# Output projection into up projection: weight tiles kept for both column halves, residual seeded in PSUM, first up operands made earlier

## The chip, the cores and the metric

The kernel runs on one core of one Trainium2 chip. A core has a matrix engine (PE, TensorE), three elementwise engines (DVE is VectorE, ACT is ScalarE, POOL is GpSimd), a queue engine (SP) that issues transfers, an on-chip memory of 128 partitions (SBUF) and an accumulator memory in eight banks (PSUM) into which PE writes. The metric is device time in microseconds (us). Before the change three timed runs gave 2550.85, 2553.93 and 2555.95 us; the median is 2553.93 us.

## What is computed

Two encoder layers over 1040 frames (16 learned ones and 1024 of input) of 1024 features, in fp32. Each layer has a mixing part and a gated feed-forward part:

```python
h = h + jnp.concatenate([o_gla, o_fox], axis=-1) @ w_out[i]
h = h + conv_ffn(rms_norm(h, ffn_norm[i]), w_up[i], conv_w[i], conv_b[i], w_down[i])
```

`conv_ffn` multiplies by `w_up` (1024 to 2 x 2816 columns), applies a causal convolution of width 3 to every column, gates one half by `silu` of the other, and multiplies by `w_down` (2816 to 1024). The change lies at the seam of the two lines: the last part of `@ w_out`, the RMS norm, and the first products with `w_up`.

## The kernel before, in words

**Layout.** Features lie on the 128 partitions, frames along the free dimension. The 1024 features are eight tiles `hT[0..7]` of 128 x 1040. Every product is made of three PE passes (`mm3`, lines 241 to 243): an fp32 operand is split into a rounded part `hi` (a cast on ACT) and the rest `lo` (a subtraction on DVE), and `hi*hi`, `lo*hi` and `hi*lo` are added up in PSUM. So every weight tile is loaded (SP, line 199), cast on ACT (line 208) and subtracted on DVE (line 210) before PE can use it; in the up projection the same is done in lines 1060 and 1061.

**The turn.** `ffn_up` begins with the output projection. Its frames are done in two halves `h = 0, 1` of 520 columns (516 and 524 in the last layer), each as two chunks of 260 (258). Eight output tiles `m` go through a half in the order of `orders`. For `m < 4` (`NSPLIT`) seven of the eight K tiles were already added during attention, so one K tile is left (6 matmuls); for `m >= 4` all eight are to be done (48 matmuls) and the residual comes from `hT[m]`. PE runs in program order. After the matmuls of one tile, `wout` adds the residual on DVE (line 1141), stores the tile (POOL, 1142), squares it on ACT (1144, 1147), adds the squares into `acc` on DVE (1148) and, in half 1, forms `gt` on ACT (1152) and `dd` on DVE (1154).

`scale(h)` sums `acc` over the partitions on PE (line 1118, tile `ssq`) and makes the reciprocal root (lines 296, 302 on ACT, 303 to 305 on DVE). `scale(0)` stands after the second tile of half 1; `scale(1)` stands after the first up product. `first_operand(k)` makes the normalised tile `k` of half 0 (DVE, 1124), and `put` splits it (ACT 1084, DVE 1085) into the operands `X[1]` (tiles 0 to 3) and `X[2]` (tiles 4 to 7).

**The up projection** is a seven-product block scheme: pairs of column blocks `j` with products `p = 1..7`. The list `seq` gives PE's order; it begins (0,2), (0,1), (1,2), (1,1), (2,2), (2,1), (0,6). Each entry is 24 matmuls. `X[2]` serves p = 2, `X[1]` p = 1; `X[6]`, `X[7]`, `X[4]`, `X[5]`, `X[3]` are made later from half 1 (`make_t2` and its neighbours, lines 1188 to 1222), all on DVE and ACT. `ensure(i)` makes the split weight operands of the entries up to `i + AHEAD` (`AHEAD` is 4).

**Buffers.** `Rings` hands out ten weight buffers w0 to w9 under three tags. While `stream` is set, `raw` turns over w0, w1, `hi` over w2 to w5 and `lo` over w6 to w9; otherwise `raw` has w0 to w3, `lo` w4 to w6, `hi` w7 to w9. The flag is cleared when the last output tile is written into the program (half 1, position 7, `m = 7`). Two output tiles (5 and 6) are kept split from half 0 to half 1 in buffers of the pool `fw`; the other six are loaded and split once per half. The entry of `seq` at an even place takes its split from `Rings`, that at an odd place from `fw`. Counting the turns of the rings in the program: the last two split chunks of `m = 7` in half 1 lie in w4 and w8, w5 and w9, and the first up operand, (0,2), takes w9 for `hi` and w4 (first layer) or w5 (second layer) for `lo`.

Larger operands lie in 39 slots of 128 x 1040 (33, and 6 more in the feed-forward part), which are handed out in the order in which they were returned. The order of the instructions on ACT, DVE, POOL and SP is made by a scheduler from readiness and program order; PE keeps the program's order.

Of the kernel before, what the change touches and what calls it, by code (L numbers as in the profile page):

```python
# [11 lines left out]
F32R = mybir.dt.float32r  # L12
BF16 = mybir.dt.bfloat16
AF = mybir.ActivationFunctionType
ALU = mybir.AluOpType
# [9 lines left out]
KD = D // 128  # L25
# [15 lines left out]
M_GK, M_GQ, M_GV, M_GR, M_REM, M_FQ, M_FK, M_FV, M_WO, M_UP = 0, 2, 4, 8, 12, 13, 17, 21, 25, 33  # L41
# [52 lines left out]
class Rings:  # L94


    def __init__(self, pool):
        self.pool, self.next, self.stream = pool, {}, False
        self.tags = {"raw": range(4), "lo": range(4, 7), "hi": range(7, 10)}, \
                    {"raw": range(2), "hi": range(2, 6), "lo": range(6, 10)}  # L100

    def tile(self, shape, dtype, tag, name, bufs=None):
        key = tag, self.stream
# [49 lines left out]
class Kern:  # L153
# [36 lines left out]
    def weights(self, src, slots=None, keep=None, vec=False):  # L190
        nc = self.nc
        nk = src.shape[1]
        parts = []
        if slots:
            HI, LO = slots
        for k0 in range(0, nk, 4):
            n = min(4, nk - k0)
            raw = self.wp.tile([128, 4, 128], F32, tag="raw", name="raw", bufs=4)
            nc.sync.dma_start(raw[:, :n, :], src[:, k0:k0 + n, :])
            if slots:  # L200
                hi, lo = HI[:, k0:k0 + 4, :], LO[:, k0:k0 + 4, :]
# [6 lines left out]
            nc.scalar.copy(hi[:, :n, :], raw[:, :n, :])  # L208
            eng = nc.gpsimd if self.att and not vec else nc.vector
            eng.tensor_tensor(out=lo[:, :n, :], in0=raw[:, :n, :], in1=hi[:, :n, :].bitcast(F32), op=ALU.subtract)  # L210
            for k in range(n):
                parts.append((hi[:, k, :], lo[:, k, :]))
        return parts
# [850 lines left out]
    def ffn_up(self, lyr, mix, hT, pp, fw, halves, o0, during_last):  # L1064
        nc, s = self.nc, self.slots
        W = halves[2]
        n = W // 2
        sl = [slice(c, c + W) for c in halves[:2]]
# [34 lines left out]
        def ensure(i):  # L1103
            while len(ops) < min(i + AHEAD + 1, len(seq)):
                ops.append(self.up_operand(lyr, *seq[len(ops)], fw, raws, len(ops) % 2))
# [19 lines left out]
            put(1 + k // 4, k % 4, h)  # L1125
        turn = {1: (), 3: (4, 5), 4: (6,), 5: (7, 0), 6: (1,), 7: (2, 3)}

        def wout(i, h):
            m = orders[h][i]
            k0 = KD - 1 if m < NSPLIT else 0  # L1130

            def f(w):
                if h == 1 and i == KD - 1:
                    self.wp.stream = False
                    ensure(0)
                ps = bank2("wo", (0, 1, 2, 0, 1, 3, 2, 1)[i] if h else i % 4)
                for k in range(len(w)):
                    for c in range(2):
                        self.mm3(ps[:, c, :n], w[k], mix[k0 + k], halves[h] + c * n, n, k == 0, k == len(w) - 1)
                x = hT[m][:, sl[h]]  # L1140
                nc.vector.tensor_tensor(out=two(x), in0=used(ps), in1=two(x), op=ALU.add)
                nc.gpsimd.dma_start(self.hm[m][:, sl[h]], x)
                if i == 0:
                    nc.scalar.activation(acc[:, sl[h]], x, AF.Square)
                else:
                    t = half(sq, i % 2)
                    nc.scalar.activation(t, x, AF.Square)
                    nc.vector.tensor_tensor(out=acc[:, sl[h]], in0=acc[:, sl[h]], in1=t, op=ALU.add)
                if h == 0:
                    return  # L1150
                if m < NSPLIT:
                    nc.scalar.mul(half(gt, m % 2), x, gain(m))
# [12 lines left out]

        def wout_weights(h, i):
            m = orders[h][i]
            if m in kept:
                return kept.pop(m)
            w = self.weights(self.wm[lyr, M_WO + m][:, KD - 1 if m < NSPLIT else 0:KD, :], keep=keep.get(m))  # L1170
            if m in keep:
                kept[m] = w
            return w
        todo = [(h, i) for h in range(2) for i in range(KD)]
        ahead = wout_weights(*todo[0])
# [2 lines left out]
            wout(this[1], this[0])(w)  # L1178
        for x in mix:
            s.put(*x)  # L1180
        s.put(gt)

        lowk, highk, t0, t1 = hT[:4], hT[4:], sl[0], sl[1]

# [578 lines left out]
```

## Time and profile before

| | before |
|---|---|
| median of three runs | 2553.93 us |
| the profiled execution's own time | 2549.59 us |
| its span | 2547.7 us |
| PE busy | 2483.9 us (97% of the span) |
| DVE busy | 1748.1 us (69%) |
| ACT busy | 1273.1 us (50%) |
| granted TensorE clock, mean | 0.994 |
| half 1 of the output projection, layer 0 | 551.3 to 577.8 us of the span |
| the same, layer 1 | 1811.4 to 1837.7 us |

A row of the timeline reads: start, duration, engine, line and operation, output tile, input tiles and shape, and in brackets how long the engine had stood idle before it and what ended that. A row of the windows view gives, for a stretch of the span, the busy time of each engine with its instruction count, the granted TensorE clock and the load of the transfers. The profiled execution lies 4.3 us below the median of the timed runs.

### The profile page before, as it was taken

Reading aid. Unit: us, or ns where it says so; the run is one execution under the profiler, and the core shown is the slowest. Engines: PE = TensorE matmul, PEld = TensorE weight load, DVE = VectorE, ACT = ScalarE, POOL = GpSimd, SP = SyncE. Lnnn points to the kernel's source line nnn. Section 1 sums busy time; section 2 is a strip of 40 time slices with the busy share of each in tenths; the row PEclk is TensorE's granted clock in tenths of the full one; section 3 lists DMA queues with packets and bytes.
Section 4 is the critical chain, followed back from the end, with each engine's and each line's share of the span. In section 5 each row is a group of like instructions: output and inputs, shape, how many; then the busy total and the mean of one; then the engine's idle time right before and its main releaser. Section 6 shows DMA issues by size and latency. Waiting matters only on the chain.

```text
span 2547.7 us, 48524 instructions
## 1 busy us (share of the span) xinstructions
PE 2483.9 (97%) x19278; PEld 2420.5 (95%) x19278; DVE 1748.1 (69%) x3389; ACT 1273.1 (50%) x2582; POOL 405.1 (16%) x580
## 2 busy tenths in 40 slices
PE   8999999999999999999999999999999999999998
PEld 7989999998999999999999899999999999999997
DVE  7655676769877777853565666777697777777535
ACT  7346666646544445641343466665464444455412
POOL 4033333210000000100210333331100000001002
PEclk9999999999999999999999999999999999999999
DMA  3232134342322224764312222142523222258622
GB/s 122 71 86 73 39 95 129 114 152 78 107 86 78 81 80 127 201 161 116 106 50 72 74 79 68 66 148 95 169 74 110 75 76 87 76 158 187 187 70 76
DMA packets 118515, 260.91 MB, mean 102 GB/s; under 512 B 14880, under 2 KB 32544, under 8 KB 118288
## 3 DMA queue, kind: packets, MB, share of 16 engines
q1 hardware_dynamic: 95136, 184.36, 23.2%
q0 software_dynamic: 22432, 72.71, 10.4%
q8 instruction: 151, 2.47, 0.4%
q10 hardware_dynamic: 720, 0.74, 0.1%
q14 instruction: 76, 0.62, 0.1%
HBM read 177.16 MB, written 67.81 MB: 96 GB/s over the span
## 4 chain that ended last, share of the span: by engine, by line
PE 65%; issue 17%; DVE 11%; DMA 3%; ACT 3%; POOL 1%; SPq 0%; DVEq 0%; POOLq 0%; ACTq 0%
PE mm L241 8%; PE mm L243 7%; PE mm L242 7%; PE up L242 5%; PE up L241 5%; PE up L243 5%; PE down L241 5%; PE down L242 5%; PE down L243 5%; PE av L741 3%; PE tr L723 2%; DVE P L694 2%; DVE x L1085 1%; PE wo L241 1%; PE S L686 1%
## 5 line engine op out<-in xcount | busy, mean ns | idle before, releaser
L241 PE MATMUL up<-x,hi 128*128 128x260 f32 (+1 forms) x2464 | 699.2, 284 | 8.0 <-ACT hi L1060 4.9
L243 PE MATMUL up<-x,hi 128*128 128x260 f32 (+1 forms) x2464 | 698.0, 283 | 2.1 <-DVE x L1085 2.1
L242 PE MATMUL up<-x,lo 128*128 128x260 f32 (+1 forms) x2464 | 698.5, 283 | 1.3 <-DVE lo L1061 1.3
L241 PEld LDWEIGHTS up<-x,hi 128*128 128x128 f32 x2464 | 466.6, 189 | 9.7 <-ACT hi L1060 5.3
L243 PEld LDWEIGHTS up<-x,hi 128*128 128x128 f32 x2464 | 467.0, 190 | 3.0 <-DVE x L1085 2.9
L242 PEld LDWEIGHTS up<-x,lo 128*128 128x128 f32 x2464 | 466.5, 189 | 2.0 <-DVE lo L1061 1.8
L1061 DVE TENSOR_TENSOR lo<-raw,hi 128x512 fp32r<-128x512 f32 x364 | 247.6, 685 | 173.4 <-ACT hi L1060 173.4
L241 PE MATMUL mm<-xh,hi 128*128 128x348 f32 (+4 forms) x1056 | 363.4, 344 | 0.0
L243 PE MATMUL mm<-xl,hi 128*128 128x348 f32 (+4 forms) x1056 | 340.0, 322 | 0.0
L242 PE MATMUL mm<-xh,lo 128*128 128x348 f32 (+4 forms) x1056 | 339.5, 321 | 0.0
L1060 ACT CAST hi<-raw 128x512 fp32r<-128x512 f32 x364 | 224.3, 620 | 145.5 <-PE up L243 84.9
L241 PEld LDWEIGHTS mm<-xh,hi 128*128 128x128 f32 x1056 | 200.0, 189 | 6.3 <-issue 5.3
L242 PEld LDWEIGHTS mm<-xh,lo 128*128 128x128 f32 x1056 | 200.0, 189 | 0.6 <-issue 0.3
L243 PEld LDWEIGHTS mm<-xl,hi 128*128 128x128 f32 x1056 | 198.8, 188 | 0.9 <-issue 0.7
L208 ACT CAST hi<-raw 128x512 fp32r<-128x512 f32 (+2 forms) x184 | 106.6, 582 | 185.0 <-PE down L243 113.0
L242 PE MATMUL down<-ah,lo 128*128 128x260 f32 (+1 forms) x704 | 198.0, 281 | 0.6 <-DVE lo L210 0.5
L243 PE MATMUL down<-al,hi 128*128 128x260 f32 (+1 forms) x704 | 198.1, 281 | 0.0
L241 PE MATMUL down<-ah,hi 128*128 128x260 f32 (+1 forms) x704 | 198.0, 281 | 0.0
L367 DVE TENSOR_TENSOR PT<-tr,PT 116x464 fp32r<-116x464 f32 (+3 forms) x240 | 122.3, 515 | 71.3 <-ACT PT L366 69.2
L702 ACT ACTIVATE P<-P,m 116x924 f32<-116x924 f32 (+4 forms) x144 | 110.5, 767 | 75.0 <-DVE m L694 69.4
L723 PE MATMUL tr<-ident,P 116*116 116x116 f32 x704 | 144.0, 268 | 2.3 <-DVE m L694 1.8
L1268 POOL DMA_DIRECT2D actd<-cv x44 | 23.6, 536 | 766.5 <-DVE cv L1267 745.5
(283 smaller groups left out, 5768.3 us busy)
## 6 DMA issues: line engine op xcount, KB each, us to landing
raw<-in_wm_dram SPq DMA_DIRECT2D x330, 256.0 KB, 2.9
raw<-in_wd_dram SPq DMA_DIRECT2D x64, 256.0 KB, 3.7
actd<-cv POOLq DMA_DIRECT2D x22, 520.0 KB, 3.0
actd<-cv POOLq DMA_DIRECT2D x22, 512.0 KB, 3.1
cb<-cd SPq DMA_DIRECT2D x16, 520.0 KB, 4.2
st<-actd SPq DMA_DIRECT2D x14, 520.0 KB, 5.1
st<-actd SPq DMA_DIRECT2D x14, 512.0 KB, 5.9
kA<-kA SPq DMA_DIRECT2D x24, 260.0 KB, 4.4
```

The costliest lines, as they stand in the source:

```text
L208: nc.scalar.copy(hi[:, :n, :], raw[:, :n, :])
L241: nc.tensor.matmul(ps, wh, xh[:, c0:c0 + n], start=first, stop=False, skip_group_check=more)
L242: nc.tensor.matmul(ps, wl, xh[:, c0:c0 + n], start=False, stop=False, skip_group_check=more)
L243: nc.tensor.matmul(ps, wh, xl[:, c0:c0 + n], start=False, stop=last, skip_group_check=more)
L367: nc.vector.tensor_tensor(out=lo, in0=src, in1=hi.bitcast(F32), op=ALU.subtract)
L686: nc.tensor.matmul(S[:rows, :n], q["qA"][e][:, qs], q["kA"][e][:, c0:k1], start=True, stop=False)
L694: nc.vector.tensor_tensor_reduce(out=x, in0=S[:rows, :n], in1=cb[:rows, c0:k1], scale=1.0, scalar=(BIG if ci == 0 else m[:rows, ci - 1:ci] ...
L702: nc.scalar.activation(x, x, AF.Exp, scale=-1.0, bias=low, accum_out=(den if nch < 3 else d2[:rows, 0:1]))
L723: nc.tensor.transpose(tr[:w, j, :rows], P[:rows, o:o + w], id_)
L741: nc.tensor.matmul(av[:, a:width], w.rearrange("p a b -> p (a b)"), x, start=(t == 0 and i == 0), stop=(t == last and i == 1))
L1060: nc.scalar.copy(hi[:, :nk, :], src[:, :nk, :])
L1061: nc.vector.tensor_tensor(out=lo[:, :nk, :], in0=src[:, :nk, :], in1=hi[:, :nk, :].bitcast(F32), op=ALU.subtract)
```

## The change

Four edits in the turn, and none elsewhere.

1. In half 0 every output weight tile is split once and kept. Tiles 0 to 3 (one K tile each) go into a slot of their own (`own`), tiles 5 and 6 into the pool `fw` as before, tiles 4 and 7 stay in the rings, which nothing else uses then. Half 1 loads and splits nothing.
2. `Rings.leave_stream` is called at the start of half 1. It gives the other layout from the ages of the buffers: `raw` gets the two raw buffers and the two `lo` buffers of tile 4, `hi` one `hi` buffer of tile 4 and both of tile 7, `lo` the other `hi` buffer of tile 4 and both `lo` buffers of tile 7.
3. The up operands (0,2) and (0,1) are written into the program at position 2 of half 1, after tile 4, and the next three at position 7.
4. For the full tiles (`m >= 4`) of half 1 the residual is copied by ACT into the PSUM banks before the matmuls (`seed`), which then add onto it. The addition of line 1141 on DVE is gone for them; the square, `dd` and a copy back into `hT` (ACT) read PSUM.

```diff
+FIRST_OPS = {2: 2, 7: 5}
...
+    def leave_stream(self):
+
+        age = {}
+        for t, ids in self.tags[True].items():
+            i = self.next.get((t, True), 0)
+            age[t] = [ids[(i + k) % len(ids)] for k in range(len(ids))]
+            self.next.pop((t, False), None)
+        (r0, r1), (h0, h1, h2, h3), (l0, l1, l2, l3) = age["raw"], age["hi"], age["lo"]
+        self.tags[False] = {"raw": [r0, r1, l0, l1], "hi": [h0, h2, h3], "lo": [h1, l2, l3]}
+        self.stream = False
...
+        place_out, seeds = (0, 1, 2, 0, 1, 3, 2, 1), {}
+        own = s.get(F32R, "wk", (128, 2 * NSPLIT, 128))
+
+        def seed(i):
+            ps = seeds[i] = bank2("wo", place_out[i])
+            nc.scalar.copy(used(ps), two(hT[orders[1][i]][:, sl[1]]))
...
             def f(w):
-                if h == 1 and i == KD - 1:
-                    self.wp.stream = False
-                    ensure(0)
-                ps = bank2("wo", (0, 1, 2, 0, 1, 3, 2, 1)[i] if h else i % 4)
+                if h == 1 and i == 0:
+                    self.wp.leave_stream()
+                if h == 1 and i in FIRST_OPS:
+                    ensure(FIRST_OPS[i] - AHEAD - 1)
+                if h == 1 and i + 1 < KD and orders[1][i + 1] >= NSPLIT:
+                    seed(i + 1)
+                ps, seeded = seeds.pop(i, None), h == 1 and m >= NSPLIT
+                if not seeded:
+                    ps = bank2("wo", place_out[i] if h else i % 4)
...
                 x = hT[m][:, sl[h]]
-                nc.vector.tensor_tensor(out=two(x), in0=used(ps), in1=two(x), op=ALU.add)
-                nc.gpsimd.dma_start(self.hm[m][:, sl[h]], x)
+                if not seeded:
+                    nc.vector.tensor_tensor(out=two(x), in0=used(ps), in1=two(x), op=ALU.add)
+                y = used(ps) if seeded else two(x)
...
-                    nc.scalar.activation(t, x, AF.Square)
+                    nc.scalar.activation(two(t), y, AF.Square)
                     nc.vector.tensor_tensor(out=acc[:, sl[h]], in0=acc[:, sl[h]], in1=t, op=ALU.add)
+                if seeded:
+                    nc.scalar.copy(two(x), y)
+                nc.gpsimd.dma_start(self.hm[m][:, sl[h]], x)
...
-                    nc.vector.scalar_tensor_tensor(out=diff(m - 4), in0=x, scalar=gain(m), in1=half(gt, m % 2),
+                    nc.vector.scalar_tensor_tensor(out=two(diff(m - 4)), in0=y, scalar=gain(m), in1=two(half(gt, m % 2)),
                                                    op0=ALU.mult, op1=ALU.subtract)
...
             m = orders[h][i]
-            if m in kept:
+            if h:
                 return kept.pop(m)
-            w = self.weights(self.wm[lyr, M_WO + m][:, KD - 1 if m < NSPLIT else 0:KD, :], keep=keep.get(m))
-            if m in keep:
-                kept[m] = w
+            src = self.wm[lyr, M_WO + m]
+            if m < NSPLIT:
+                w = self.weights(src[:, KD - 1:KD, :], [own[:, j:j + 1, :] for j in (m, NSPLIT + m)])
+            else:
+                w = self.weights(src, keep=keep.get(m))
+            kept[m] = w
             return w
```

More of the change, by code (lines that the diff above doesn't have):

```diff
@@ L98, in __init__ @@
         self.pool, self.next, self.stream = pool, {}, False
-        self.tags = {"raw": range(4), "lo": range(4, 7), "hi": range(7, 10)}, \
-                    {"raw": range(2), "hi": range(2, 6), "lo": range(6, 10)}
+        self.tags = [{"raw": range(4), "lo": range(4, 7), "hi": range(7, 10)},
+                     {"raw": range(2), "hi": range(2, 6), "lo": range(6, 10)}]
+    def leave_stream(self):
[7 more added lines that the diff above has]
+        self.stream = False
     def tile(self, shape, dtype, tag, name, bufs=None):
@@ L200, in weights @@
             if slots:
-                hi, lo = HI[:, k0:k0 + 4, :], LO[:, k0:k0 + 4, :]
+                hi, lo = HI[:, k0:k0 + n, :], LO[:, k0:k0 + n, :]
             elif keep:
@@ L1132, in f @@
             def f(w):
-                if h == 1 and i == KD - 1:
-                    self.wp.stream = False
-                    ensure(0)
-                ps = bank2("wo", (0, 1, 2, 0, 1, 3, 2, 1)[i] if h else i % 4)
+                if h == 1 and i == 0:
[7 more added lines that the diff above has]
+                    ps = bank2("wo", place_out[i] if h else i % 4)
                 for k in range(len(w)):
                     for c in range(2):
-                        self.mm3(ps[:, c, :n], w[k], mix[k0 + k], halves[h] + c * n, n, k == 0, k == len(w) - 1)
+                        self.mm3(ps[:, c, :n], w[k], mix[k0 + k], halves[h] + c * n, n,
+                                 k == 0 and not seeded, k == len(w) - 1, seeded)
                 x = hT[m][:, sl[h]]
-                nc.vector.tensor_tensor(out=two(x), in0=used(ps), in1=two(x), op=ALU.add)
-                nc.gpsimd.dma_start(self.hm[m][:, sl[h]], x)
+                if not seeded:
+                    nc.vector.tensor_tensor(out=two(x), in0=used(ps), in1=two(x), op=ALU.add)
+                y = used(ps) if seeded else two(x)
                 if i == 0:
-                    nc.scalar.activation(acc[:, sl[h]], x, AF.Square)
+                    nc.scalar.activation(two(acc[:, sl[h]]), y, AF.Square)
                 else:
                     t = half(sq, i % 2)
-                    nc.scalar.activation(t, x, AF.Square)
+                    nc.scalar.activation(two(t), y, AF.Square)
                     nc.vector.tensor_tensor(out=acc[:, sl[h]], in0=acc[:, sl[h]], in1=t, op=ALU.add)
+                if seeded:
+                    nc.scalar.copy(two(x), y)
+                nc.gpsimd.dma_start(self.hm[m][:, sl[h]], x)
                 if h == 0:
@@ L1180, in ffn_up @@
             s.put(*x)
-        s.put(gt)
+        s.put(gt, own)
         lowk, highk, t0, t1 = hT[:4], hT[4:], sl[0], sl[1]
```

## The prediction

> **What bounds the kernel now.** I read the page first: PE is busy 97% of the span, so a change is worth only what PE stands still, or runs at a lower clock, at the place it touches. The first group of the up projection is also the costliest one in idle time, and most of that is a wait for a cast of line 1060.
>
> ```profile
> PE 2483.9 (97%) x19278; PEld 2420.5 (95%) x19278; DVE 1748.1 (69%) x3389; ACT 1273.1 (50%) x2582; POOL 405.1 (16%) x580
> ...
> L241 PE MATMUL up<-x,hi 128*128 128x260 f32 (+1 forms) x2464 | 699.2, 284 | 8.0 <-ACT hi L1060 4.9
> ```
>
> Then the windows view cuts layer 0 around the turn, with the last row from layer 1:
>
> ```profile
> 551.30:577.80 26.50, 26.50 (x219) 26.20 (x217) 22.78 (x38) 14.95 (x28) 5.49 (x10) 1.00 0.63 196
> 577.80:588.00 10.20, 7.42 (x34) 6.97 (x34) 8.66 (x15) 4.56 (x9) 0.82 (x2) 0.67 0.22 80
> 588.00:604.00 16.00, 16.00 (x137) 16.00 (x136) 15.96 (x27) 9.64 (x18) 0.00 (x0) 1.00 0.06 18
> ...
> 619.00:630.00 11.00, 8.35 (x61) 7.30 (x60) 11.00 (x19) 6.75 (x11) 0.89 (x1) 1.00 0.38 102
> ...
> 1837.70:1848.50 10.80, 7.39 (x37) 6.93 (x37) 9.10 (x15) 5.87 (x12) 1.08 (x2) 0.68 0.21 73
> ```
>
> In half 1 PE is full. In the 10 us behind it PE is busy 7.42 of 10.20 us, does only 34 matmuls (a full 10 us holds about 85, by the next row) and has a clock of 0.67. Some 30 us later there is a second hole, 2.65 us, at full clock, while DVE has no idle time at all. PE's timeline gives the turn itself, layer 0 and then layer 1:
>
> ```profile
> 557.37 1.04 PE L1118 MATMUL ssq<-r,ones 128*128 128x260 f32 x4
> 558.06 0.48 PE L241 MATMUL wo<-mh,hi 128*128 128x260 f32 x1
> ...
> 565.45 0.28 PE L241 MATMUL wo<-mh,keep 128*128 128x260 f32 x1
> ...
> 571.93 0.28 PE L241 MATMUL wo<-mh,hi 128*128 128x260 f32 x1
> ...
> 577.55 0.28 PE L243 MATMUL wo<-ml,hi 128*128 128x260 f32 x1
> 579.68 0.38 PE L241 MATMUL up<-x,hi 128*128 128x260 f32 x1 [1.85 <-ACT hi L1060]
> 581.00 0.58 PE L242 MATMUL up<-x,lo 128*128 128x260 f32 x1 [0.93 <-DVE lo L1061]
> ...
> 585.93 0.42 PE L243 MATMUL up<-x,hi 128*128 128x260 f32 x1
> 586.15 1.43 PE L1118 MATMUL ssq<-r,ones 128*128 128x260 f32 x4
> 587.22 0.47 PE L241 MATMUL up<-x,hi 128*128 128x260 f32 x1
> ...
> 1837.47 0.28 PE L243 MATMUL wo<-ml,hi 128*128 128x258 f32 x1
> 1840.78 0.58 PE L241 MATMUL up<-x,hi 128*128 128x258 f32 x1 [3.03 <-ACT hi L1060]
> ...
> 1847.37 0.47 PE L241 MATMUL up<-x,hi 128*128 128x258 f32 x1
> ```
>
> From the last output matmul to the first one of the second up product (0,1) PE takes 587.22 - 577.55 = 9.67 us in layer 0, and 1847.37 - 1837.47 = 9.90 us in layer 1. Between lie one matmul step, 24 matmuls of (0,2) and the four of `ssq`. At full pace a step is 0.119 us (54 steps from 565.45 to 571.93 in the rows: 48 of tile 6 and 6 of tile 3, 6.48 us, 0.12 each), and `ssq` took 558.06 - 557.37 = 0.69 us: 0.12 + 24 x 0.12 + 0.69 = 3.7 us. **So the turn loses 6.0 us in layer 0 and 6.2 us in layer 1, 12.2 us in all**; that is the ceiling of what filling it can bring. The loss has two parts: the wait for the split of (0,2), about 3.3 us, and a stretch at half clock behind it (0.38 to 0.58 us per row instead of 0.28; 585.93 to 586.15 is a step of 0.22), 22 steps x 0.1 = 2.2 us.
>
> The page "TensorE: Matmul & The Clock Gate" of the Trainium skill (Part 1) has the clock halve after an idle window of about 3.4 us and return after a busy one of the same length. By that estimate the slow stretch would cost 3.4 x 0.45 = 1.5 us instead of 2.2, and the ceiling would be 10.8 us; the rows above show 5 us of it, and I go by them.
>
> **Why (0,2) is late.** By the buffer count in the text above, its `hi` lies in w9, which tile 7 reads until PE's last output matmul at 577.55. The cast can run only then, and it stands in ACT's queue behind a square, a `gt` and a cast:
>
> ```profile
> 565.90 1.30 ACT L1084 CAST x<-h 128x520 fp32r<-128x520 f32 x2 [2.35 <-DVE h L1124]
> ...
> 572.04 1.14 ACT L1084 CAST x<-h 128x520 fp32r<-128x520 f32 x2
> ...
> 575.20 0.60 ACT L1060 CAST hi<-raw 128x512 fp32r<-128x512 f32 x1
> 577.34 0.64 ACT L1147 ACTIVATE sq<-h 128x520 f32<-128x520 f32 x1 [1.54 <-DVE h L1141]
> 577.88 0.71 ACT L1152 ACTIVATE gt<-h,vec 128x520 f32<-128x520 f32 x1
> 578.50 0.61 ACT L1084 CAST x<-h 128x520 fp32r<-128x520 f32 x1
> 579.02 0.61 ACT L1060 CAST hi<-raw 128x512 fp32r<-128x512 f32 x1
> ```
>
> DVE is behind as well. From 560.12 it hardly stops (windows, then its timeline):
>
> ```profile
> 560.12:586.00 25.88, 23.10 (x172) 22.69 (x172) 25.83 (x41) 14.25 (x25) 4.16 (x7) 0.89 0.56 178
> 586.00:624.50 38.50, 36.56 (x290) 35.36 (x289) 36.93 (x61) 24.86 (x45) 0.90 (x1) 0.99 0.22 63
> ```
>
> ```profile
> 560.12 0.69 DVE L210 TENSOR_TENSOR lo<-raw,hi 128x512 fp32r<-128x512 f32 x1 [0.52 <-ACT hi L208]
> ...
> 574.05 0.69 DVE L1085 TENSOR_TENSOR x<-h,x 128x520 fp32r<-128x520 f32 x1
> ...
> 576.56 0.69 DVE L1141 TENSOR_TENSOR h<-wo,h 128x520 f32<-128x520 f32 x1
> 577.17 0.75 DVE L1124 SCALAR_TENSOR_TENSOR h<-h,vec,r 128x520 f32<-128x520 f32 x1
> ...
> 582.07 0.69 DVE L1141 TENSOR_TENSOR h<-wo,h 128x520 f32<-128x520 f32 x1
> ...
> 587.53 0.69 DVE L1061 TENSOR_TENSOR lo<-raw,hi 128x512 fp32r<-128x512 f32 x1 [1.54 <-ACT hi L1060]
> ```
>
> The add of tile 7 runs at 582.07, 4.2 us after PE gave the tile. An add takes 0.69 us but the next starts 0.61 us after it (576.56, 577.17), so I count 0.61 each.
>
> **The change part by part, per layer.**
>
> *Kept tiles.* Half 1 loses the split of tiles 4 and 7 (four casts and four subtractions of 128 x 512) and of four small ones: on DVE 4 x 0.61 + 4 x 0.2 = 3.2 us, about as much on ACT, and twelve transfers on SP become six. Only the two subtractions of tile 7 (560.12 and one 2.4 us later) lie in DVE's full stretch: **1.2 us**. The others fell in slack and bring nothing. Writing tiles 0 to 3 into the slot costs what the ring cost. The slot makes 39 of 39 in use; it last held attention's keys and its first tile is needed only at PE's second position, 5.7 us into half 0, so I cost it at nothing; without that cover it would be a wait in half 0.
>
> *Operands sooner.* (0,2) takes two buffers of tile 4, which PE has left at 557.4; its two raw loads can go once tile 3 of half 0 is split, more than 20 us ahead of the turn, and SP has nothing else then (the two issues move past no other load). Cast and subtraction (0.61 each) are done by about 560. (0,1) has its own buffers in `fw`. That takes the wait for the split out of the turn, and **1.2 us** of DVE work (two subtractions) out of the full stretch into earlier slack. (1,2) takes the buffers of tile 7's first chunk, free halfway through tile 7, some 9 us before PE wants it.
>
> *Seeds.* DVE loses the adds of tiles 4 to 7, three of them in the full stretch: **1.8 us**. For tile 7 the square no longer waits for a DVE add that ran 4.2 us late. ACT gains four seeds and four copies back. The copy from PSUM has a row, the seed only a narrower one, and the bounds are that one and its double:
>
> ```profile
> L1244 ACT COPY hu<-up 128x520 f32<-128x520 f32 x44 | 26.1, 593 | 63.8 <-PE up L243 63.6
> ...
> L1611 ACT COPY mm<-h 128x256 f32<-128x256 f32 x7 | 2.3, 364 | 0.0
> ```
>
> A seed is 0.36 to 0.73 us, I take 0.6, since both rows with 520 columns lie near it. That is 8 x 0.6 = 4.8 us more on ACT, less what the splits gave back: about 17 to 18 busy of 26.5 us in half 1, against 14.95. It hides under PE as long as the order on ACT is good. A seed waits for its bank: that of tile 7 for the add of tile 2. Behind a waiting seed stand the casts of `X`, and PE waits for the seed. POOL's stores now wait for ACT's copy; behind them is only a transfer needed at p = 6.
>
> *What is late next.* With (0,2) ready and `X[2]` complete (its last split was at 574.05), PE begins at 577.7 and is at `ssq` 2.9 us later, at 580.6, which needs tile 7's square (ACT, 578.5) and its addition (DVE, 0.61). Then `X[1]` is wanted from 581.4 on. DVE's work up to there ended at 586 with the add of tile 7 on it; 1.2 + 1.2 + 1.8 = 4.2 us less gives 581.8, and the idle 1.54 us at 587.53 came of the slow PE. So DVE just about arrives with PE, and the gain is bounded from both sides: 4.2 us by DVE's saved work alone, 6.1 us by the turn's own loss. DVE's full stretch runs on into the second hole, so a DVE that is 4.2 to 6 us earlier meets a PE that is as much earlier, and that hole stays as it is within about 1.5 us. I take the middle, 5.2 us per layer, **10.4 us in all**.
>
> 2549.59 - 10.4 = 2539.2 us for the profiled execution; against the median of the runs, 2553.93, it is **2543.5 us**. Its own range: 2 x 4.2 = 8.4 saved, to 12.2 and 1.5 per hole, 15.2: 2538.7 to 2545.5.
>
> **The rivals.**
>
> *DVE sets the pace all the way* (2547.7 us). If the two operands' subtractions stay in the full stretch, DVE gains 3.1 us per layer, 6.2 in all; PE starts up in time but stands at `ssq`, at `X[1]` and longer in the second hole. For it: DVE's 25.83 of 25.88 us. Against it: the slack before 560.
>
> *Two readers of a seeded bank* (2550.1 us). ACT's square and copy and DVE's `dd` now all read the same PSUM tile. If `dd` stands on DVE until ACT is through, 0.64 + 0.59 less some overlap, about 1.1 us each, three times in the full stretch, the saving of 5.2 shrinks to 1.9 us per layer. Against it: other DVE work is ready to go first. The page "PSUM — Partial Sum Buffer" of the Trainium skill (Terms) says that two engines must not be on one bank at once, reads included, which would force such an order; no run here shows what comes of it.
>
> *The change doesn't do what it says* (2552 us): the cast of (0,2) is still put behind others on ACT, and only the half-clock stretch shrinks a little, 1 us per layer.
>
> *Seeds late* (2561 us, the other side). In the rows above ACT does two casts of `X` at 565.90 that waited for DVE, and is busy with casts until 575.8. If the seed of tile 6 stands behind the first, it ends at 567.2 + 0.6 = 567.8 against 565.45, a stop of 2.3 us; behind the second, tile 7's ends at 576.4 against 571.93, a stop of 4.4 us, and by layer 1 a stop of 3 us costs the half-clock stretch too, 2.2 us. 8.9 - 5.2 = 3.7 us more per layer. It decides once seeds stop PE for more than 5.2 us per layer, clock included.
>
> **How the numbers follow.** My forecast 0.53, DVE all the way 0.20, two readers 0.10, no effect 0.06, seeds late 0.11. A change below 0.2%, 5.1 us, can't be told from none. Faster than that: 0.53 and three quarters of 0.20, 0.68. Slower: 0.11. The rest, 0.21, is no change. The range goes from the low end of my own, 2538.5, past the first two rivals to 2553, near the no-effect case; it leaves out the late seeds and the tails.
>
> **What would show it.** Right: PE's first up matmul within 0.5 us of the last output one, clock 1.00 in the first 10 us of up in both layers, no cast of line 1060 before it, line 1141 with 24 instructions instead of 32, `ssq` of `scale(1)` within 2 us of the end of (0,2). Wrong: PE idle before a seeded tile with ACT as releaser; a second hole that grew by what the turn gave; a clock still below 0.9 at the turn.

## The result and the profile after

| | before | after |
|---|---|---|
| median of six runs, same comparison | 2552.39 us | 2539.99 us |
| ratio, 95% interval | | 0.9951 [0.9937, 0.9965] |
| profiled execution's own time | 2549.59 us | 2536.52 us |
| its span | 2547.7 us | 2534.7 us |
| granted TensorE clock, mean | 0.994 | 0.996 |

The change makes the kernel 12.4 us faster by the medians and 13.07 us by the profiled executions; the prediction was 10.4 us. Line numbers have moved: `mm3` is 253 to 255 now, the split of the up operands 1072 (cast) and 1073 (subtraction), the first combination of raw weight blocks 1055 (was 1043), the split of `X` 1096 and 1097, `ssq` 1130, the residual add 1167, seed and copy back 1145 and 1176, `dd` 1183, the weight split in the output projection 220 and 222.

On the page, the up projection's first group no longer has its wait for the cast (4.9 of 8.0 us before). What is left is for the most part two waits for DVE:

```profile
PE 2477.9 (98%) x19278; PEld 2415.6 (95%) x19278; DVE 1737.0 (69%) x3365; ACT 1275.9 (50%) x2582; POOL 405.5 (16%) x580
...
L253 PE MATMUL up<-x,hi 128*128 128x260 f32 (+1 forms) x2464 | 697.2, 283 | 2.1 <-DVE hg L1275 1.3
L255 PE MATMUL up<-x,hi 128*128 128x260 f32 (+1 forms) x2464 | 695.9, 282 | 2.4 <-DVE x L1097 2.4
```

PE's timeline at the turn, layer 0 and then layer 1 (start, duration, engine, operation):

```profile
575.59 0.28 PE L255 MATMUL wo<-ml,hi 128*128 128x260 f32 x1
575.71 0.28 PE L253 MATMUL up<-x,hi 128*128 128x260 f32 x1
...
578.57 1.04 PE L1130 MATMUL ssq<-r,ones 128*128 128x260 f32 x4
579.26 0.47 PE L253 MATMUL up<-x,hi 128*128 128x260 f32 x1
...
1828.63 0.28 PE L255 MATMUL wo<-ml,hi 128*128 128x258 f32 x1
1828.75 0.28 PE L253 MATMUL up<-x,hi 128*128 128x258 f32 x1
...
1832.32 0.47 PE L253 MATMUL up<-x,hi 128*128 128x258 f32 x1
```

The first up matmul follows the last output matmul in one step, 0.12 us. From the last output matmul to (0,1) it is 579.26 - 575.59 = 3.67 us and 1832.32 - 1828.63 = 3.69 us; before it was 9.67 and 9.90. So the turn gives back 6.0 and 6.2 us, all that the prediction called the ceiling. The windows view shows no slow clock there (first row, and the last row for layer 1), and the second hole about 37 us later still open (second row, PE 9.61 of 12.00 us beside a full DVE):

```profile
575.80:586.00 10.20, 10.20 (x84) 10.08 (x83) 9.21 (x16) 5.93 (x12) 0.54 (x1) 1.00 0.23 79
...
609.00:621.00 12.00, 9.61 (x74) 8.78 (x73) 12.00 (x21) 7.40 (x14) 0.89 (x1) 1.00 0.44 124
1828.90:1839.70 10.80, 10.80 (x89) 10.69 (x88) 9.68 (x17) 6.34 (x13) 0.54 (x1) 1.00 0.23 75
```

ACT's timeline shows where the pieces went: the cast of (0,2) is done 22 us ahead of the turn, and a seed takes 0.58 us. The last two rows are tile 7's square and copy back:

```profile
552.92 0.61 ACT L1072 CAST hi<-raw 128x512 fp32r<-128x512 f32 x1
...
566.04 0.58 ACT L1145 COPY wo<-h 128x520 f32<-128x520 f32 x1
...
576.57 0.60 ACT L1173 ACTIVATE sq<-wo 128x520 f32<-128x520 f32 x1
577.07 0.58 ACT L1176 COPY h<-wo 128x520 f32<-128x520 f32 x1
```

DVE's timeline after begins its unbroken stretch at 555.68, and ends it with the last low parts of `X` at 619.5:

```profile
555.68 0.69 DVE L1073 TENSOR_TENSOR lo<-raw,hi 128x512 fp32r<-128x512 f32 x1 [3.87 <-issue]
...
577.92 0.75 DVE L1183 SCALAR_TENSOR_TENSOR dd<-wo,vec,gt 128x520 f32<-128x520 f32 x1
...
580.89 0.69 DVE L1073 TENSOR_TENSOR lo<-raw,hi 128x512 fp32r<-128x512 f32 x1 [0.99 <-ACT hi L1072]
...
617.05 2.52 DVE L1097 TENSOR_TENSOR x<-h,x 128x520 fp32r<-128x520 f32 x4
619.49 0.69 DVE L1275 TENSOR_TENSOR hg<-up,hg 128x520 f32<-128x520 f32 x1
```

The same stretch in both kernels (in the kernel before from 558.10, 2 us ahead of the 560.12 of the prediction), first as a row of the windows view of before, then of after (columns: stretch, length, busy time and instructions of PE, PEld, DVE, ACT, POOL, clock, transfers):

```profile
558.10:628.15 70.05, 65.29 (x504) 63.44 (x502) 67.87 (x111) 40.25 (x71) 6.48 (x10) 0.95 0.36 112
```

```profile
555.60:619.57 63.97, 62.24 (x506) 61.13 (x505) 62.83 (x102) 41.61 (x73) 6.46 (x10) 1.00 0.34 104
```

DVE does 102 instructions there instead of 111, 67.87 - 62.83 = 5.0 us less, and idles 1.1 us instead of 2.2. Which nine went, by the groups of before and then of after:

```profile
L1061 DVE TENSOR_TENSOR lo<-raw,hi 128x512 fp32r<-128x512 f32 x17 | 11.2, 683 | 1.5 <-ACT hi L1060 1.5
L1141 DVE TENSOR_TENSOR h<-wo,h 128x520 f32<-128x520 f32 x7 | 4.8, 691 | 0.0
L1043 DVE TENSOR_TENSOR raw<-raw,raw 128x512 f32<-128x512 f32 x7 | 4.7, 681 | 0.0
L210 DVE TENSOR_TENSOR lo<-raw,hi 128x512 fp32r<-128x512 f32 (+1 forms) x3 | 1.7, 556 | 2.0 <-ACT hi L208 2.0
```

```profile
L1073 DVE TENSOR_TENSOR lo<-raw,hi 128x512 fp32r<-128x512 f32 x16 | 10.6, 681 | 4.9 <-issue 3.9 <-ACT hi L1072 1.0
L1055 DVE TENSOR_TENSOR raw<-raw,raw 128x512 f32<-128x512 f32 x6 | 4.0, 679 | 0.0
L1167 DVE TENSOR_TENSOR h<-wo,h 128x520 f32<-128x520 f32 x3 | 2.1, 689 | 0.0
```

Four adds, the three weight subtractions (one of them a small one of 0.29 us that the start of the window cuts), one subtraction and one combination for up operands. The last two ran at 538.21 and 536.39, inside half 0: with no output weights to load in half 1, raw weights of the up projection arrive that early.

### The profile page after: what moved, and what is told of

It reads as the page before. It is cut to its first block, busy times and chain, and to the rows that moved or that the text cites. A ratio compares the mean times of both kernels' runs of the same rounds, so it can differ in the third digit from the quotient of the medians.

```text
span 2534.7 us, 48450 instructions
## 1 busy us (share of the span) xinstructions
PE 2477.9 (98%) x19278; PEld 2415.6 (95%) x19278; DVE 1737.0 (69%) x3365; ACT 1275.9 (50%) x2582; POOL 405.5 (16%) x580
## 3 DMA queue, kind: packets, MB, share of 16 engines
q0 software_dynamic: 22432, 72.71, 10.4%
## 4 chain that ended last, share of the span: by engine, by line
PE 53%; issue 31%; DVE 8%; DMA 3%; ACT 2%; POOL 2%; SPq 0%; DVEq 0%; POOLq 0%; ACTq 0%
PE mm L253 8%; PE mm L255 7%; PE mm L254 7%; PE down L253 5%; PE down L254 5%; PE down L255 5%; PE av L753 3%; PE tr L735 2%; DVE P L706 2%; PE wo L253 1%; PE wo L255 1%; PE wo L254 1%; PE S L698 1%; DVE cv L1268 1%; PE S L699 1%
## 5 line engine op out<-in xcount | busy, mean ns | idle before, releaser
L220 ACT CAST hi<-raw 128x512 fp32r<-128x512 f32 (+1 forms) x160 | 96.8, 608 | 151.0 <-PE down L255 117.1
```

## The experiments

**The measure.** The parts of the span that no edit touches add up to between 1534 and 1543 us from one profiled execution to the next, as much as the effects. So beside the medians stands the *region*, from the first output matmul to the last up matmul, both layers added. Its *front* runs to the `ssq` behind (0,2), the rest is *behind*. In two executions of the changed kernel the region is the same within 0.1 us; of every other kernel one execution is measured. Each ratio is against executions of the kernel before made beside that run, whose median lay between 2549.77 and 2554.43 us. Medians and regions do not always agree: against the changed kernel "no seeds" is 6.4 us slower by the medians and 3.2 us by the region, "operands at position 0" 3.2 and 0.0 us. For these differences no run shows a cause, so effects of a few us rest on the region alone.

| kernel | median us | ratio to before, 95% interval | front | behind | region |
|---|---|---|---|---|---|
| before | 2552.39 | | 123.1 | 890.4 | 1013.5 |
| changed | 2539.99 | 0.9951 [0.9937, 0.9965] | 111.2 | 888.8 | 1000.0 |
| no seeds | 2546.41 | 0.9972 [0.9961, 0.9982] | 112.9 | 890.2 | 1003.2 |
| late buffers | 2539.60 | 0.9941 [0.9929, 0.9953] | 114.5 | 885.4 | 999.8 |
| operands at position 7 | 2540.20 | 0.9949 [0.9937, 0.9961] | 111.2 | 888.8 | 999.9 |
| seeds only | 2547.72 | 0.9988 [0.9977, 0.9999] | 122.5 | 887.6 | 1010.1 |
| kept tiles only | 2545.32 | 0.9971 [0.9960, 0.9982] | 115.5 | 889.5 | 1005.0 |
| late raw buffer | 2547.99 | 0.9978 [0.9969, 0.9988] | 124.2 | 883.4 | 1007.6 |
| `X[7]` on POOL | 2544.05 | 0.9963 [0.9948, 0.9977] | 111.2 | 895.4 | 1006.6 |
| all eight seeded | 2540.69 | 0.9946 [0.9933, 0.9959] | 111.2 | 889.8 | 1001.0 |
| operands at position 0 | 2543.20 | 0.9954 [0.9940, 0.9967] | 111.2 | 888.8 | 1000.0 |
| all seeded, operands at 0 | 2541.56 | 0.9954 [0.9940, 0.9968] | 111.2 | 889.1 | 1000.3 |
| `X[7]` without subtraction | 2535.28 | 0.9930 [0.9909, 0.9952] | 111.2 | 884.1 | 995.3 |

**The changed kernel again**, with no edit.

> The changed kernel once more, beside the variants. In its first profile the span is 13.0 us shorter than before. By my reading 12.2 us of that are the two turns, about 1.2 us the two second holes, and the rest (2.0 us less ahead of layer 0's output projection, 2.1 us more in layer 1's down projection) is the spread between executions. Then this profile again shows no stop of PE at the turn in either layer, clock 1.00 there, and stage lengths elsewhere that differ from the first profile by up to 2 us with no fixed sign. Rival: the 2.0 us and the 2.1 us belong to the change, and both come back within 0.3 us. Time expected 2537 to 2543 us.

2540.17 us, ratio 0.9948 [0.9936, 0.9960], region 1000.1. The region gains 13.5 us against before: 11.9 in front, 1.6 behind.

**No seeds.**

```diff
-                if h == 1 and i + 1 < KD and orders[1][i + 1] >= NSPLIT:
-                    seed(i + 1)
-                ps, seeded = seeds.pop(i, None), h == 1 and m >= NSPLIT
+                seeded = False
```

> The changed kernel with the seeds undone: the full tiles of half 1 get their residual from DVE's addition again; kept tiles and early operands stay. My theory (the buffers of the first operand open the turn, DVE's relief only lets it arrive in time behind it): PE still goes from the last output matmul into (0,2) within 0.3 us and keeps its clock, but DVE has four additions more, 2.4 us, so PE stands at ssq, at X[1] or in the second hole for 2 to 2.5 us per layer: 4 to 5 us slower than the changed kernel, 7 to 8 us faster than before. Rival 1 (buffers alone do it): within 1.5 us of the changed kernel. Rival 2 (the seeds do it): PE stands before (0,2) again and the clock halves, 10 us or more slower than the changed kernel.

Region 1003.2, so seeds are worth 3.1 us, less than the 4 to 5 expected. PE enters (0,2) at once here too; it stops at `ssq`, for the sum of squares that DVE's late adds hold up:

```profile
583.58 1.14 PE L1130 MATMUL ssq<-r,ones 128*128 128x260 f32 x4 [1.14 <-DVE r L1172]
```

**Late buffers.** (0,2) takes a `hi` and a `lo` buffer of tile 7's last chunk, which PE reads to the end, as it read w9 in the kernel before.

```diff
-        self.tags[False] = {"raw": [r0, r1, l0, l1], "hi": [h0, h2, h3], "lo": [h1, l2, l3]}
+        self.tags[False] = {"raw": [r0, r1, l0, l1], "hi": [h3, h2, h0], "lo": [l3, l2, h1]}
```

> The changed kernel with one edit: the first up operand takes the two ring buffers of tile 7's last chunk, which PE reads until the last output matmul, and the last of the five takes tile 4's. Everything else, DVE's relief too, stays. My theory: the cast of (0,2) can't begin before PE's end; cast and subtraction, 0.6 us each, with their hand-offs stop PE for 1.3 to 3 us per layer; if the stop reaches about 3 us the clock halves as before and costs 2.2 us more. 3 to 10 us slower than the changed kernel in all. Rival (DVE's and ACT's relief filled the turn, not the buffers): PE stops less than 0.5 us per layer, within 1.5 us of the changed kernel.

PE's timeline, the turn and then the second hole:

```profile
578.57 0.39 PE L253 MATMUL up<-x,hi 128*128 128x260 f32 x1 [0.71 <-ACT hi L1072]
579.40 0.39 PE L254 MATMUL up<-x,lo 128*128 128x260 f32 x1 [0.44 <-DVE lo L1073]
```

```profile
617.49 0.39 PE L253 MATMUL up<-x,hi 128*128 128x260 f32 x1 [0.48 <-ACT x L1096]
618.41 0.39 PE L255 MATMUL up<-x,hi 128*128 128x260 f32 x1 [0.42 <-DVE x L1097]
```

The turn stops for 1.15 us at full clock; front is 3.3 us longer over both layers, behind 3.5 us shorter, and the region stays. The buffer of (0,2) costs a short stop, and the second hole swallows it. **The buffer, which the prediction put first as the reason why (0,2) is late, explains 1.15 us of a wait of 2.78 us in layer 0 (1.05 of 3.41 us in layer 1) and, with DVE relieved, none of the lost time.**

**Operands at position 7.** All first operands are written into the program with the last output tile.

```diff
-FIRST_OPS = {2: 2, 7: 5}
+FIRST_OPS = {7: 5}
```

> The changed kernel with the first two up operands written into the program at position 7 of half 1 like the other three, in the same buffers as in the changed kernel. My theory (the buffers decide, and the scheduler moves a ready cast forward whatever its place in the program): both casts still run well ahead of PE's end, no stop at the turn, within 1.5 us of the changed kernel. Rival (the place in the program decides): the cast of (0,2) stands behind position 6's work on ACT and DVE, PE stops 1 to 3 us per layer, 2 to 10 us slower than the changed kernel.

The same as the changed kernel: with the buffers free, the scheduler takes (0,2) forward by itself.

**Seeds only.** The kernel before with edit 4 alone.

```diff
+                if h == 1 and i + 1 < KD and orders[1][i + 1] >= NSPLIT:
+                    seed(i + 1)
+                ps, seeded = seeds.pop(i, None), h == 1 and m >= NSPLIT
...
-                nc.vector.tensor_tensor(out=two(x), in0=used(ps), in1=two(x), op=ALU.add)
+                if not seeded:
+                    nc.vector.tensor_tensor(out=two(x), in0=used(ps), in1=two(x), op=ALU.add)
...
```

> The kernel before with the seeds alone: no tile kept beyond the two of before, buffers and place of the up operands as before. Measure: the length from the first output matmul to the last up matmul, both layers together (before 1013.5, changed 1000.0, changed without seeds 1003.2, late buffers 999.8 us). Theory now (DVE's unbroken stretch from tile 4 to the second hole sets the end of this length, and a short stop at the turn is swallowed by the hole): three to four adds of 0.61 us less per layer, 2 to 2.5 us, so 1008 to 1010 us, whatever the turn looks like. Rival (the buffer of (0,2) makes the turn, and the turn is the loss): the turn stays as long as before, 1012 to 1014 us.

Region 1010.1, a gain of 3.4 us, and here the rival "seeds late" is seen: PE waits for ACT's seed (line 1132 in this kernel) in each layer.

```profile
576.40 0.39 PE L241 MATMUL wo<-mh,hi 128*128 128x260 f32 x1 [2.22 <-ACT wo L1132]
...
1837.15 0.39 PE L241 MATMUL wo<-mh,hi 128*128 128x258 f32 x1 [3.81 <-ACT wo L1132]
```

With the splits of half 1 still on ACT the seeds come late. In the changed kernel, and with late buffers or late positions as well, no seed stops PE. Of the edits that "seeds only" lacks, that leaves edit 1 to keep the seeds in time; a kernel with edits 1 and 4 alone was not run.

**Kept tiles only**: no seeds, late buffers and operands at position 7 together, which leaves edit 1 and the new buffer layout that it needs.

```diff
-FIRST_OPS = {2: 2, 7: 5}
+FIRST_OPS = {7: 5}
...
-        self.tags[False] = {"raw": [r0, r1, l0, l1], "hi": [h0, h2, h3], "lo": [h1, l2, l3]}
+        self.tags[False] = {"raw": [r0, r1, l0, l1], "hi": [h3, h2, h0], "lo": [l3, l2, h1]}
...
-                ps, seeded = seeds.pop(i, None), h == 1 and m >= NSPLIT
+                seeded = False
```

> The changed kernel without the seeds, without the early place of the operands, and with the first up operand in the buffers of tile 7's last chunk: only the kept tiles (and the buffer layout that they need) are left. Theory now (DVE's stretch): the same DVE work as in the run without seeds but for one subtraction that can't go ahead, so 1003 to 1005 us for the length from first output to last up matmul; the stop at the turn, 1 to 3 us per layer, comes back out of the second hole unless the clock halves. Rival (without the right buffers the turn of before is back, with its halved clock): 1009 to 1013 us.

Region 1005.0, a gain of 8.5 us. With the 3.4 of "seeds only" that is 11.9 of the 13.5. Edit 1 brings the most of what was tried alone, though the prediction gave its subtractions 1.2 us per layer against 1.8 for the adds: with it the turn waits 0.71 + 1.36 us in layer 0, and no half clock follows. Edits 2 and 3 together bring 1.8 us where there are no seeds (1005.0 to 1003.2); with the seeds, undoing either of them costs nothing (999.8 and 999.9).

**Late raw buffer.** (0,2) loads into the raw buffer `l3` that tile 7's last chunk holds until PE is through, so that it is as late as in the kernel before, while DVE keeps its savings.

```diff
-        self.tags[False] = {"raw": [r0, r1, l0, l1], "hi": [h0, h2, h3], "lo": [h1, l2, l3]}
+        self.tags[False] = {"raw": [r0, l3, l0, l1], "hi": [h0, h2, h3], "lo": [h1, l2, r1]}
```

> The changed kernel with one raw buffer of the first up operand swapped for a buffer of tile 7's last chunk, so that the transfer of (0,2)'s weights itself starts only after the last output matmul. DVE's and ACT's work is the changed kernel's. The stop at the turn should be a transfer (2.8 us), a cast and a subtraction: 4 to 5 us per layer, with the clock halved behind it as before (about 2 us more). Theory now (the second hole, 2.6 us per layer, swallows what the turn loses up to its own size, the rest is paid): 1000 + 2 x (6.5 - 2.6) = 1006 to 1009 us for the length. Rival (any loss at the turn is paid in full): 1012 to 1014 us. Rival (PE's turn doesn't matter at all): 1000 us.

```profile
583.68 0.58 PE L253 MATMUL up<-x,hi 128*128 128x260 f32 x1 [3.09 <-ACT hi L1072]
584.65 0.58 PE L254 MATMUL up<-x,lo 128*128 128x260 f32 x1 [0.38 <-DVE lo L1073]
...
625.00 0.39 PE L255 MATMUL up<-x,hi 128*128 128x260 f32 x1 [0.31 <-DVE x L1097]
```

This is the run that separates the two causes. Front is 124.2 us, as long as before (123.1), half clock included. But behind is 883.4 against 890.4: the second hole is all but gone (the last row is all of it in layer 0). The stop adds 13.0 us in front, 5.4 come back behind, and the region loses 7.6. In the kernel before the same stop found DVE late by as much, so nothing came back.

**`X[7]` on POOL.** The four subtractions for `X[7]`, all behind `ssq`, go to POOL.

```diff
-                put(7, k, diff(k))
+                put(7, k, diff(k), nc.gpsimd)
```

> The changed kernel with the four subtractions that make the low part of operand X[7] moved from DVE to POOL, which stands idle there; nothing else. Theory now (DVE's stretch sets the end): 4 x 0.61 = 2.4 us less DVE work per layer closes most of the second hole, 995 to 997 us for the length, 3 to 5 us off the time. It falls short if POOL, at some 1.3 us each, makes X[7] late for PE, or slows DVE: 999 us or more. Rival (the second hole is not DVE's work but the order of its last steps): 1000 us.

Worse: 1006.6 instead of the 995 to 997 expected. POOL's and DVE's timelines:

```profile
590.77 9.92 POOL L1097 TENSOR_TENSOR x<-dd,x 128x520 fp32r<-128x520 f32 x4 [8.63 <-ACT x L1096]
```

```profile
594.88 1.21 DVE L1097 TENSOR_TENSOR x<-h,x 128x520 fp32r<-128x520 f32 x1
596.01 1.80 DVE L1226 TENSOR_TENSOR h<-dd,h 128x520 f32<-128x520 f32 x1
597.74 3.50 DVE L1073 TENSOR_TENSOR lo<-raw,hi 128x512 fp32r<-128x512 f32 x2
```

DVE's instructions beside POOL's take up to 1.80 us instead of 0.69: these four last 6.3 us, from 594.88 to the start of the next at 601.16, where four of 0.61 would be 2.4, and the difference, 3.8 us, is more than the 2.4 us that POOL takes off DVE. PE stops for it, and again for later splits, with half clock behind:

```profile
601.90 0.39 PE L255 MATMUL up<-x,hi 128*128 128x260 f32 x1 [1.88 <-DVE x L1097]
603.15 0.58 PE L253 MATMUL up<-x,hi 128*128 128x260 f32 x1 [0.45 <-ACT hi L1072]
```

**All eight seeded.** The four one-K tiles get seeds as well, so the other four adds of half 1 go from DVE; all of them run ahead of `ssq`.

```diff
-                if h == 1 and i + 1 < KD and orders[1][i + 1] >= NSPLIT:
+                if h == 1 and i == 0:
+                    seed(0)
+                if h == 1 and i + 1 < KD:
                     seed(i + 1)
-                ps, seeded = seeds.pop(i, None), h == 1 and m >= NSPLIT
+                ps, seeded = seeds.pop(i, None), h == 1
...
-                    nc.scalar.mul(half(gt, m % 2), x, gain(m))
+                    nc.scalar.mul(two(half(gt, m % 2)), y, gain(m))
```

> The changed kernel with all eight tiles of half 1 seeded, the four small ones too: DVE loses four more additions per layer, three of them inside its unbroken stretch, ACT gains eight copies. Theory (the length from first output to last up matmul is DVE's end of the stretch plus a constant, 403.5 us per layer in every run so far): 3 x 0.61 = 1.8 us less per layer, 996 to 997 us for the two lengths together against 1000.0, 3 to 4 us off the time. It falls short if a seed comes late on ACT, which then has about 22 of 26.5 us busy: PE would show a wait for ACT before an output tile. Rival (the seeds have given what they can, since PE no longer waits at the turn): 1000 us.

1001.0 instead of 996 to 997. DVE's timeline of layer 0 shows the saved work as idle time, 2.32 us where the changed kernel has 0.99:

```profile
581.92 0.69 DVE L1073 TENSOR_TENSOR lo<-raw,hi 128x512 fp32r<-128x512 f32 x1 [2.32 <-ACT hi L1072]
```

The cast it waits for stands on ACT behind the copy of the first up product, so DVE waits for PE there. Work taken off DVE ahead of `ssq` is worth nothing any more. The 1.0 us more of the region is all in layer 1 and behind the second hole, whose last wait there ends as long after the last output matmul as in the changed kernel (44.5 us); its cause is not shown.

**Operands at position 0, alone and with all eight seeded** (the second adds the diff above to this one).

```diff
-FIRST_OPS = {2: 2, 7: 5}
+FIRST_OPS = {0: 2, 7: 5}
```

> The changed kernel with the first two up operands written into the program at position 0 of half 1, not 2. The operand (0,1) has its buffers free by then, and DVE stands idle for 3.9 us just before its unbroken stretch begins. Theory: if the scheduler puts the subtraction of (0,1) there, the stretch is 0.61 us shorter per layer and the two lengths come to 998.8 us; if it keeps the order, 1000.0. Nothing above 1000.5.

> Both at once: all tiles seeded and the first operands at position 0. Theory (DVE's saved work adds up): 995 to 996 us for the two lengths, 4 to 5 us off the changed kernel's time. Rival (ACT, with eight copies and the earlier casts, becomes late with a seed): 998 us or more, with a wait of PE for ACT in half 1.

1000.0 and 1000.3: no gain. Alone, the earlier place leaves the order as it was, with the same idle 3.87 us before the stretch. The subtraction that opens the stretch is that of (0,2), and it starts when PE has just left tile 4, whose buffer its `lo` takes; that of (0,1) had run in half 0 already (538.21 in the changed kernel). With all eight seeded DVE has the idle time of the run before (2.33 us).

**`X[7]` without its subtraction.**

```diff
-                put(7, k, diff(k))
+                hi_, lo_ = (X[7][i][k // 2].t[:, k % 2, :W] for i in range(2))
+                nc.scalar.copy(hi_, diff(k))
+                nc.scalar.copy(lo_, diff(k))
```

> The low part of X[7] is made by a copy on ScalarE of the first difference instead of VectorE's subtraction; the subtraction is left out, so that low part is wrong and the run prices time alone. Four VectorE operations of about 0.61 us per layer go, 2.4 us, all of them behind the sum of squares, and nothing goes to GpSimd. Measured is the region from the first output-projection matmul to the last up matmul, both layers added (1000.0 us in the changed kernel). Theory: since the change, VectorE's unbroken work from the sum of squares to the second hole sets the region, and only work behind the sum of squares counts: 1000.0 - 2 x 2.4 = 995 to 996 us, up to 997 if ScalarE's four added copies come late; the idle time of TensorE some 30 us behind the turn, about 3 us per layer, shrinks by as much. Rival: the second hole is not VectorE's work but something else that comes at a fixed time behind the turn: 1000 us and the same idle time.

The region is 995.3, as the theory had it, all of it behind (-4.7 us). PE's one wait of the second hole in layer 0, where the changed kernel has four:

```profile
613.24 0.39 PE L255 MATMUL up<-x,hi 128*128 128x260 f32 x1 [0.42 <-DVE x L1097]
```

So the second hole is DVE's work between `ssq` and the last low part of `X`. Behind is 884.1 us here and 883.4 with the late raw buffer, near the same floor by two ways: PE with hardly a wait. No kernel that computes the whole of the reference has a region clearly below that of the changed one.

## Why the prediction was right, and where it was not

**The direction and most of the size.** 10.4 us were forecast, against 12.4 measured by the medians (8.9 to 16.1 by the interval of the ratio) and 13.5 by the region. The likeliest case stood for a saving of 8.4 to 15.2 us, and it is the one that came: PE enters the up projection without a stop, and DVE is earlier by as much.

**The ceiling was reached.** "The turn loses 6.0 us in layer 0 and 6.2 us in layer 1, 12.2 us in all" came back to 0.1 us, with the half-clock stretch in it. The lower ceiling of 10.8 us, which the prediction worked out from the Trainium skill ("TensorE: Matmul & The Clock Gate", Part 1), does not agree with that; the rows do.

**The term that was mis-sized** is "4.2 us less" of DVE's work. Measured in layer 0: nine instructions fewer, 5.0 us, where I had counted seven. One add more, and the cut end of a third weight subtraction, fell in the stretch, which is taken here 2 us longer at its start; of the two up-operand subtractions that were to leave it one did, and a combination of raw blocks. Beside that DVE idles 1.0 us less, and its stretch starts 0.5 us sooner after the first output matmul (32.56 us instead of 33.05). 5.0 + 1.0 + 0.5 = 6.6 us, which is the region's gain in that layer, 505.53 - 498.93 = 6.6. The middle of the two bounds (5.2 us per layer) was a choice without a reason for the middle: the lower bound was too low, and the upper one, 6.1 us, held for the turn alone (6.0 and 6.2 us). The regions gained more, 6.6 and 6.9 us, because a part of the gain lies behind the turn, where the prediction had allowed up to 1.5 us per layer in its range.

**The cause that was wrong in part** is "Why (0,2) is late": the `hi` in w9, with the queue on ACT named second. Putting a buffer of tile 7 back ("late buffers") costs 1.15 us of waiting in layer 0 instead of 2.78 (1.85 + 0.93), and nothing in the end. The rest of the wait went with the work that edits 1 and 4 take off DVE and ACT: with either of them alone and the old or the late buffers, it is 0.59 + 0.48 us ("seeds only") and 0.71 + 1.36 us ("kept tiles only") in layer 0. The rows of the kernel before show what held the queue on ACT. In layer 0 the square at 577.34, three places ahead of the cast of (0,2), had waited 1.54 us for DVE's add. In layer 1 two other casts had waited 1.76 us for a transfer of raw weights, and the cast of (0,2) came behind them, at 1840.11:

```profile
1836.88 1.14 ACT L1060 CAST hi<-raw 128x512 fp32r<-128x512 f32 x2 [1.76 <-DMA raw<-in_wm_dram]
...
1840.11 0.61 ACT L1060 CAST hi<-raw 128x512 fp32r<-128x512 f32 x1
```

How much of the wait each of these brings was not tried. For the time, DVE is what counts: in the kernel before, PE's waits 43 to 47 us behind the last output matmul are for the operands that DVE and ACT make. "Late raw buffer" shows the other half: the same stop without DVE's lateness costs 7.6 us, not 13.5.

**"What is late next."** The second hole was to stay "within about 1.5 us": behind `ssq` the kernel gains 1.0 us in layer 0 (444.43 to 443.40) and 0.5 in layer 1. Right, and now with its cause: DVE's work.

**The rivals.** "DVE sets the pace all the way" had the mechanism right in part: DVE's work sets where the second hole ends, as `X[7]` without its subtraction shows, but PE stands neither at `ssq` nor at `X[1]`. Its size was wrong: it left the operands' work in the stretch, which went out of it in part, and counted three adds for four. "Two readers of a seeded bank" was not seen: in the rows above ACT has read tile 7 until 577.65 and `dd` starts at 577.92, after other work, with no idle time of DVE; for the other seeded tiles too `dd` starts 0.2 to 0.7 us after ACT is through, and DVE is never idle for it. The PSUM page of the Trainium skill ("PSUM — Partial Sum Buffer", Terms) says that two engines must not be on a bank at once; in these rows they are not, so no run shows what an overlap would do. "Seeds late" does not occur in the changed kernel, and does in "seeds only", which lacks edit 1. "Doesn't do what it says" is refuted by the cast at 552.92.

**Costs taken as bounded.** A seed was 0.58 us (0.6 taken, between 0.36 and 0.73), and no seed stops PE.

## What to carry to other kernels

When one engine is busy with hardly a break over a long stretch, as DVE here, look for the last place where PE waits for it: a stop of PE inside the stretch is given back there up to the size of that wait, and only what comes off that engine's work shortens the time, until it begins to wait for PE itself. The engine or buffer named at the stop is therefore not yet the cause. To tell them apart, put the stop back and keep the savings, and measure a stretch cut out of the trace when the rest of the kernel scatters as much as the effect.

## What the hardware showed that was not expected

**DVE and POOL side by side.** The four POOL subtractions, 128 x 520 with both inputs in SBUF, took 9.92 us (4.76 the first, by the instructions of that line, and about 1.75 each of the others), and DVE's instructions beside them, also with two SBUF inputs, up to 1.80 us instead of 0.69. During attention POOL does 52 such subtractions of 128 x 512 in 1.29 us each on the mean. While the first one ran DVE kept its pace; afterwards both engines took about 1.75 us per instruction. (In layer 1 POOL's four took 2.24, 1.76, 1.76 and 1.62 us, so the 4.76 of the first is not a fixed price.) The Trainium skill, "SBUF — State Buffer" (Who interferes with whom), says that a VectorE instruction with two SBUF inputs contends with a GpSimd instruction that reads SBUF, and that the order of issue decides which of the two blocks. The run agrees in kind; which instruction held which isn't shown.

**When the clock halves.** "Seeds only" has a single stop in each layer, 2.22 and 3.81 us (rows above). The windows view of that kernel around the first, and behind the second:

```profile
573.90:579.00 5.10, 2.88 (x24) 2.68 (x23) 4.68 (x8) 5.03 (x10) 0.95 (x2) 1.00 0.67 174
...
1837.00:1842.00 5.00, 4.84 (x27) 4.85 (x28) 5.00 (x9) 2.68 (x6) 0.54 (x1) 0.66 0.28 109
```

A stop of 2.22 us kept the full clock, one of 3.81 us did not. The Trainium skill, "TensorE: Matmul & The Clock Gate" (Part 1), sets an idle window of about 3.4 us; these two rows agree. Two others do not. The stop of 3.09 us of "late raw buffer" in layer 0 was shorter, and the clock behind it was 0.50:

```profile
584.00:589.00 5.00, 4.62 (x21) 4.36 (x21) 3.28 (x5) 0.62 (x1) 0.00 (x0) 0.50 0.29 105
```

In the kernel before, 1.85 and 0.93 us of waiting with a matmul between them (rows in the prediction) halved the clock too, so the idle time need not be in one piece. In "kept tiles only" 0.71 and 1.36 us did not halve it. How long an idle time must be is not shown.
